# One encoder layer on one core: state-space rows without their 1 / rms, a written order of the output products and logits, and expert weights loaded from the first branch product on

## Chip, cores and metric

The kernel runs on one core of a Trainium2 chip, as one program and one launch. The metric is the device time of an execution in microseconds; each time is the median of several runs. The core has five engines that run side by side, each through its own list of instructions in order: TensorE (PE; its weight loads are PEld), VectorE (DVE), ScalarE (ACT), GpSimd (POOL) and SyncE (SP), which issues nearly all DMAs. Matrix products land in PSUM, eight banks of 128 rows of 512 fp32 values; everything else lies in SBUF.

## The reference

One layer of a streaming encoder on 256 tokens of width 1024, all in fp32. After a norm, one wide projection feeds two branches. One is sparse attention. The other is a state-space scan (SSD): 2048 channels in 4 groups, which is multiplied by SiLU of a gate z, normed within each group of 512 channels and scaled:

```python
yf = y * silu(z)
yg = yf.reshape(..., 4, 512)
yg = yg * rsqrt(mean(yg * yg, axis=-1) + 1e-6)
y_ssd = yg.reshape(..., 2048) * ssd_norm

merged = sigmoid(gate_a) * (y_attn @ w_attn_branch) + sigmoid(gate_b) * (y_ssd @ w_ssd_branch)
x = x + merged @ w_out
x = x + hier_moe(rmsnorm(x, ffn_norm), ...)
```

The last part routes each token to one of 4 expert groups and in it to 2 of 8 SwiGLU experts (hidden width 256). Every one of the 32 experts has weights of 3 MiB, 96 MiB in all.

## The kernel before

**Order of the work.** The program is written with a framework that plans the order of each engine's instructions from a simulated time line. Instructions of one engine may change places; where an order is wanted, it is forced by `pin` (behind everything written before on that engine), by `tc.issue_after(i)` (behind instruction i) and by a raised priority (`HP`).

**Weights of the dense part** come in 38 chunks of up to 8 slices of 128 rows. `next_w` asks for the next chunk one chunk ahead. SyncE loads it as raw fp32 (line 141) into 4 buffers "R"; ScalarE casts each slice to the high half (line 152), and GpSimd or VectorE, in turns, subtract it from the raw value for the low half (line 156), into buffers "S" that hold 6 slices. A product takes three passes: high by high, high by low, low by high (`PASSES`). `wide_chunk` multiplies both token tiles t = 0, 1 of 128 rows with 512 columns, 48 matmuls, into two PSUM banks; t = 1 runs `LAG` slices behind t = 0.

**State-space stage** (`ssd_x`, `ssd_e`, `ssd_y`, `ssd_tail`, lines 706 to 784). For each group g and half q, `ssd_y` computes yg, 256 channels by 256 tokens, with channels on the rows, and adds their squares into ysum. `ssd_tail(g)` sums ysum over the rows (ps_n), computes 1 / rms of each token as a column nv, turns that into a row that stands on all 128 partitions by two small matmuls with the identity (ps_r, line 775), multiplies yg by the gain and by that row, and splits it into the high and low half of yT[g] (lines 781 to 784). The four yT are held in the four large buffers "L".

**Branch products** (lines 825 to 847). Four chunks (i, c): i is the half of the channels (groups 2i and 2i + 1), c the half of the 1024 output columns. Each product, of 8 slices of channels in one sum, is multiplied by (gate table + 1) on its way out of PSUM (line 832) and added to `tab`, on GpSimd for i = 0, on VectorE for i = 1; then it is transposed into mT (tag "G").

**Output product and logits** (lines 869 to 912). w_out comes as one chunk of 512 columns and two of 256. For each slice c of 256 columns: x1 = x + product (VectorE), squares (ScalarE), two transposes for each token tile (ps_hf), a scaling to xT by ScalarE and VectorE, and the router's logits (ps_lg). The last slice is done by token tile. `warm2` puts matmuls with no use behind given instructions; 11 stand behind the last logit and 3 behind each rank.

**Routing and experts.** `route(t)` is a chain of some 13 VectorE operations with one small matmul (ps_rk) that ends in the slot matrix Dm. Eight passes q of 4 experts follow: `gather(k, n)` picks the tokens of slice k by matmuls with Dm (ps_g) and scales them into xg; `gate_up(k)` multiplies four experts at once into pgu; then the down product (py) and the sum over experts (acc). `GA` is the order of gathers and products in the first pass; `combine` computes the weights of the experts' outputs, and its VectorE work is queued behind the last Dm.

**Expert loads.** The weights are 96 tiles of 1 MiB, 12 in each pass. `prefetch(tags)` issues the next tiles on SyncE into buffers that are named by a letter: 7 E, 2 H, 2 A, 3 X, 4 L, 2 made of R, 3 of S and 2 of G, 25 in all, and then the same ring again. Each load is queued behind the last raw load that has been written, and waits for its buffer: X lies over memory of the state-space stage, L over the yT. Before: two X after chunk (1, 0), an X and an L after (1, 1), then an L with each of three slices of the output product; R, S and G come after the logits.

Of the kernel before, what the change touches and what calls it, by code (L numbers as in the profile page):

```python
# [20 lines left out]
P = 128  # L21
# [27 lines left out]
def block_kernel(ctx, tc, xin, idn, ngain, catt, cprep, cssd, cmoe, cwr, wsm, wwide, win, wgu, wdn, out, dbg=None):  # L49
# [185 lines left out]
    def mm3(regions):  # L235


        for k in range(KD):
            for j, (ps, lhs, rhs) in enumerate(regions):
                for i, (a, b) in enumerate(PASSES):  # L240
                    pe.matmul(ps, lhsT=lhs[k][:, a], rhs=rhs[k][:, b],  # L241
                              start=j == 0 and k == 0 and i == 0,
                              stop=j == len(regions) - 1 and k == KD - 1 and i == 2)

# [438 lines left out]
    snorm = C("snorm")  # L683
    yT = [bigt([P, 2, 4, T], F32R, f"yT{g}") for g in range(4)]
# [53 lines left out]
    def ssd_y(g, q):  # L738
# [3 lines left out]
        st_[g, q, "yg"] = yg  # L742
# [3 lines left out]
        for h2 in range(2):  # L746
# [9 lines left out]
            dve.tensor_tensor(yg[:, h2, :], yg[:, h2, :], zs[:, h2, :], op=ALU.mult)  # L756
        sq = zs_t[g, q]
# [7 lines left out]
    def ssd_tail(g):  # L765
# [4 lines left out]
        r = ssd.tile([P, 2], F32, tag="nv", name="nv")  # L770
# [6 lines left out]
        for q in range(2):  # L777
            yg = st_[g, q, "yg"]
            for b in range(2):
                ct = 4 * g + 2 * q + b  # L780
# [44 lines left out]

    for i in range(2):
        for c in range(2):
            ps = wide_chunk("S", yT[2 * i:2 * i + 2], LAG)
            for t in range(2):
# [16 lines left out]
            if i:  # L846
                prefetch(PF1[2 * c] + PF1[2 * c + 1])
# [21 lines left out]
    for c in range(4):  # L869
        if c == 0:  # L870
            pw = wide_chunk("o", mT, 4)
            for t in range(2):
                dve.scalar_tensor_tensor(x1[:, t, 0:512], pw[t], 0.5, x_sb[:, t, 0:512], op0=ALU.mult, op1=ALU.add)
        elif c == 2:
            ps = tm_chunk(next_w(), mT, "o")
        elif c == 3:
            ps = [pmm.tile([P, T], F32, tag="mm", name=f"ps_o{t}") for t in range(2)]
            regions = tm_regions(next_w(), mT, ps)
        prefetch(PFO[c])
        o = slice(256 * c, 256 * c + 256)  # L880
        if c == 3:

            dve.tensor_reduce(pre, ssq[:, :, 0:3], axis=AX.X, op=ALU.add)
            dve.tensor_scalar(pre, pre, D * EPS, None, op0=ALU.add)
        for ts in ((0,), (1,)) if c == 3 else ((0, 1),):
            tt = slice(ts[0], ts[-1] + 1)
            nt = len(ts)
            if c == 3:
                mm3(regions[ts[0]:ts[0] + 1])
            phf = pacc.tile([P, 2, nt, P], F32, tag=f"acc{ts[0]}1", name="ps_hf")  # L890
            xT = mo2.tile([P, 2, nt, P], F32, tag="y", name="xT")
            if c > 1:
                dve.scalar_tensor_tensor(x1[:, tt, o], ps[ts[0]].unsqueeze(1) if c == 3 else ps, 0.5, x_sb[:, tt, o],
                                         op0=ALU.mult, op1=ALU.add)
# [416 lines left out]
```

## Time and profile before

| | |
|---|---|
| median of 3 runs | 583.62 us (583.45 to 583.9) |
| profiled execution | 585.1 us |
| its span, first to last instruction | 583.3 us |
| busy: PE, DVE, ACT, POOL | 552.6, 330.9, 271.8, 239.5 us |
| read from device memory | 157.54 MB, 272 GB/s over the span |
| granted TensorE clock, mean | 0.987 |

The profile is of one execution. Busy time of TensorE is modelled: matmuls overlap, so a busy share near 1 means that no gap was seen. A DMA share of 1 means that the core's 16 DMA engines were all busy. Names are those of the program: ps_S is the branch product, ps_o the output product, ps_lg the logits, ps_hf the transposes ahead of them, ps_g the gather, pgu the expert product, we an expert tile, w_raw and w_hl the raw and the split dense weights. L156 is line 156 of the kernel; "<-" after an idle time names what ended it.

### The profile page before, as it was taken

The numbers are of one execution on the slowest core, as the hardware profiler recorded it, in microseconds if no ns is written. First come the engines' busy times: TensorE is split into PE (matmuls) and PEld (weight loads), VectorE is DVE, ScalarE is ACT, GpSimd is POOL, SyncE is SP. The second block draws the span as 40 slices with busy tenths as digits, with TensorE's granted clock in tenths as the row PEclk, the third lists the DMA queues.
The fourth block names the chain that finished last, engine by engine and source line by source line (L and its number), as shares of the span: only waits on it lengthen the run. The fifth ranks groups of instructions, "written<-read, shape, count | busy, mean of one in ns | idle before, by whom it ended". The sixth has DMA issues, their size and how long they took to land.

```text
span 583.3 us, 9898 instructions
## 1 busy us (share of the span) xinstructions
PE 552.6 (95%) x3605; PEld 400.6 (69%) x3605; DVE 330.9 (57%) x689; ACT 271.8 (47%) x633; POOL 239.5 (41%) x254
## 2 busy tenths in 40 slices
PE   8999989999999999999999999999998898988976
PEld 5878768798898999898878888964453452433512
DVE  3659975999996778989695657451111121111101
ACT  7567557757987877878764436410000000000001
POOL 4687584775844456656567745210000000000000
PEclk9999999999999999999999999999989997999989
DMA  7755244453435488645568589989999999999993
GB/s 272 250 162 169 103 147 146 144 174 124 128 122 186 149 323 334 217 149 185 208 194 300 177 307 389 405 344 417 419 417 408 420 417 421 409 415 421 420 407 123
DMA packets 35123, 159.27 MB, mean 273 GB/s; under 512 B 4096, under 2 KB 5760, under 8 KB 25856
## 3 DMA queue, kind: packets, MB, share of 16 engines
q1 hardware_dynamic: 33776, 157.30, 71.8%
q10 hardware_dynamic: 1296, 1.30, 0.7%
q8 instruction: 30, 0.49, 0.3%
q14 instruction: 21, 0.17, 0.1%
HBM read 157.54 MB, written 1.05 MB: 272 GB/s over the span
## 4 chain that ended last, share of the span: by engine, by line
PE 69%; DMA 12%; DVE 9%; issue 4%; POOL 3%; ACT 3%; SPq 0%; ACTq 0%; POOLq 0%; DVEq 0%
PE ps_S L294 8%; PE pgu L1037 6%; PE ps_xs L241 6%; PE ps_g L294 6%; DMA we<-wdn 5%; DMA we<-wgu 5%; PE ps_z L241 5%; PE py L1097 4%; PE ps_A L294 4%; PE acc L1112 4%; PE ps_g L1030 4%; PE ps_q L294 3%; PE ps_o L241 2%; PE ps_o L294 2%; PE ps_iq L294 2%
## 5 line engine op out<-in xcount | busy, mean ns | idle before, releaser
L156 POOL TENSOR_TENSOR w_hl<-w_raw,w_hl 128x512 fp32r<-128x512 f32 (+1 forms) x101 | 141.6, 1406 | 81.8 <-ACT w_hl L152 66.5
L152 ACT CAST w_hl<-w_raw 128x512 fp32r<-128x512 f32 (+1 forms) x212 | 125.7, 620 | 46.4 <-PE ps_S L294 18.5
L156 DVE TENSOR_TENSOR w_hl<-w_raw,w_hl 128x512 fp32r<-128x512 f32 (+1 forms) x111 | 100.4, 911 | 38.7 <-ACT w_hl L152 38.1
L1055 POOL TENSOR_TENSOR dc<-Dm,cmr 128x128 f32<-128x128 f32 x16 | 6.1, 401 | 143.5 <-DVE Dm L960 137.4
L1037 PE MATMUL pgu<-we,xg 128*32 128x512 f32 x512 | 60.2, 603 | 3.9 <-DMA we<-wgu 3.9
L241 PE MATMUL ps_z<-hT,w_hl 128*128 128x256 f32 x384 | 51.7, 286 | 0.0
L241 PE MATMUL ps_xs<-hT,w_hl 128*128 128x256 f32 x384 | 50.7, 285 | 0.0
L241 PEld LDWEIGHTS ps_z<-hT,w_hl 128*128 128x128 f32 x384 | 47.8, 190 | 2.0 <-issue 2.0
L241 PEld LDWEIGHTS ps_xs<-hT,w_hl 128*128 128x128 f32 x384 | 47.6, 191 | 2.1 <-issue 2.1
L294 PE MATMUL ps_g<-w_hl,gT 128*128 128x512 f32 x192 | 48.1, 399 | 0.0
L294 PE MATMUL ps_S<-w_hl,yT 128*128 128x512 f32 x192 | 44.6, 391 | 0.0
L1033 DVE TENSOR_TENSOR xg<-ps_g,cmoe 128x512 f32<-128x512 f32 (+2 forms) x18 | 11.3, 631 | 57.4 <-PE ps_g L1030 57.4
L1030 PEld LDWEIGHTS ps_g<-Dm,x_sb 128*128 128x128 f32 x256 | 31.0, 191 | 14.9 <-issue 9.7
L294 PEld LDWEIGHTS ps_g<-w_hl,gT 128*128 128x128 f32 x192 | 34.9, 188 | 9.3 <-DVE w_hl L156 1.0
L294 PEld LDWEIGHTS ps_S<-w_hl,yT 128*128 128x128 f32 x192 | 35.8, 188 | 7.4
L1037 PEld LDWEIGHTS pgu<-we,xg 128*32 128x32 f32 x512 | 15.1, 110 | 37.1 <-issue 26.1
L1097 PE MATMUL py<-we,aTt 128*32 128x512 f32 (+1 forms) x272 | 35.8, 616 | 3.8 <-DVE aTt L1083 2.1
L1108 ACT COPY y<-py 128x512 f32<-128x512 f32 (+1 forms) x9 | 4.8, 539 | 66.9 <-PE py L1097 66.9
L1075 DVE SCALAR_TENSOR_TENSOR ac<-th,pgu 128x256 f32<-128x256 f32 x8 | 3.4, 421 | 57.5 <-ACT th L1073 57.5
L1112 PE MATMUL acc<-y,dcT 128*128 128x512 f32 (+1 forms) x68 | 32.6, 606 | 0.9 <-DVE y L1110 0.8
L1030 PE MATMUL ps_g<-Dm,x_sb 128*128 128x128 f32 x256 | 33.4, 280 | 0.0
L1073 ACT ACTIVATE th<-pgu,rs 128x256 f32<-128x256 f32 x8 | 3.8, 474 | 55.1 <-PE pgu L1037 55.1
(296 smaller groups left out, 968.9 us busy)
## 6 DMA issues: line engine op xcount, KB each, us to landing
we<-wgu SPq DMA_DIRECT2D x55, 1024.0 KB, 13.8
w_raw<-wwide SPq DMA_DIRECT2D x60, 512.0 KB, 3.9
w_raw<-win SPq DMA_DIRECT2D x44, 512.0 KB, 3.9
we<-wdn SPq DMA_DIRECT2D x17, 1024.0 KB, 17.4
we<-wdn SPq DMA_DIRECT2D x28, 512.0 KB, 12.0
we<-wgu SPq DMA_DIRECT2D x18, 512.0 KB, 10.2
x_sb<-xin SPq DMA_DIRECT2D x2, 512.0 KB, 4.4
we<-wdn SPq DMA_DIRECT2D x4, 256.0 KB, 11.5
```

The source lines that it names most:

```text
L152: return act.copy(self.hl[i][:, 0], self.raw[i])
L156: return eng.tensor_sub(hl[:, 1], self.raw[i], hl[:, 0].bitcast(F32))
L241: pe.matmul(ps, lhsT=lhs[k][:, a], rhs=rhs[k][:, b], start=j == 0 and k == 0 and i == 0, stop=j == len(regions) - 1 and k == KD - 1 and i ...
L294: pe.matmul(ps[t], lhsT=lhs[t][k][:, a], rhs=w[k][:, b], start=k == 0 and i == 0, stop=k == KD - 1 and i == 2)
L1030: pe.matmul(ps[:, kk, :], lhsT=x1[:, t, (k + kk) * P:(k + kk + 1) * P], rhs=Dm[:, t].rearrange("p e j -> p (e j)"), start=t == 0, stop=t == 1)
L1033: dve.tensor_tensor(xg[:, ks, :], ps, fgain[:, ks].unsqueeze(2).to_broadcast([P, n, P]), op=ALU.mult)
L1037: i = pe.matmul(pgu[32 * e:32 * e + 32, :], lhsT=xg[:, k, 32 * e:32 * e + 32], rhs=wg[k][e], start=k == 0, stop=k == KD - 1, tile_position ...
L1055: pool.tensor_tensor(dc[:, t], Dm[:, t], cmr[:, t, 4 * q:4 * q + 4].unsqueeze(2).to_broadcast([P, 4, NSLOT]), op=ALU.mult)
L1073: act.activation(th, pgu[:, 0:256], AF.Tanh, scale=rs)
L1097: i_py = pe.matmul(py[32 * e:32 * e + 32, :], lhsT=aTt[:, f, 32 * e:32 * e + 32], rhs=wd[2 * n + f][e][:, c], start=f == 0, stop=f == 1, t ...
L1108: act.copy(y, py)
L1112: pe.matmul(acc[t][n][:, c], lhsT=dcT[:, t * P:(t + 1) * P], rhs=y, start=False, stop=q == 7 and c.stop == 512)
```

## The change

**1 / rms.** `ssd_tail` keeps the column only, in a small tile `rg` of all groups. `ssd_y` now makes both halves of yT itself, without 1 / rms, by four operations on ScalarE and four on VectorE for each group. The branch product keeps the two groups of a chunk apart, four PSUM banks instead of two, and 1 / rms is a factor of each row on the way out:

```diff
+        hl = yT[g][:, :, 2 * q:2 * q + 2]
+        for b in range(2):
+            ct = 4 * g + 2 * q + b
+            act.activation(hl[:, 0, b], yg[:, b], AF.Copy, scale=snorm[:, ct:ct + 1])
+            dve.scalar_tensor_tensor(hl[:, 1, b], yg[:, b], snorm[:, ct:ct + 1], hl[:, 0, b].bitcast(F32),
+                                     op0=ALU.mult, op1=ALU.subtract)
...
-        ps_r = paux.tile([P, T], F32, tag="n", bufs=1, name="ps_r")
-        for t in range(2):
-            pe.matmul(ps_r[:, t * P:(t + 1) * P], lhsT=r[:, t:t + 1].to_broadcast([P, P]), rhs=ident,
-                      start=True, stop=True)
...
-                dve.scalar_tensor_tensor(yg[:, b, :], yg[:, b, :], snorm[:, ct:ct + 1], ps_r, op0=ALU.mult, op1=ALU.mult)
-            hl = yT[g][:, :, 2 * q:2 * q + 2]
-            act.copy(hl[:, 0], yg)
-            dve.tensor_sub(hl[:, 1], yg, hl[:, 0].bitcast(F32))
...
+    for t in range(2):
+        for c in range(2):
+            pool.tensor_scalar(tab[t, c][:, 1], tab[t, c][:, 1], 1.0, None, op0=ALU.add)
...
+                    if kk % 4 == 0:
+                        pss[t, g] = (pacc.tile([P, 512], F32, tag=f"acc{t}1", name="ps_S") if g
+                                     else pmm.tile([P, 512], F32, tag="mm", name="ps_S"))
+                    for a, b in PASSES:
+                        pe.matmul(pss[t, g], lhsT=src[kk][:, a, t * P:(t + 1) * P], rhs=w[kk][:, b],
+                                  start=kk % 4 == 0 and (a, b) == PASSES[0], stop=kk % 4 == 3 and (a, b) == PASSES[2])
+            for g, t in ((0, 0), (0, 1), (1, 0), (1, 1)):
...
-                dve.scalar_tensor_tensor(m, tb, 1.0, ps[t], op0=ALU.add, op1=ALU.mult)
-                if i == 0:
+                dve.scalar_tensor_tensor(m, pss[t, g], rg[:, 2 * i + g, t:t + 1], tb, op0=ALU.mult, op1=ALU.mult)
+                if i == 0 or g == 0:
                     pool.tensor_add(ta, m, ta)
```

**Expert loads.** The tiles and the ring are the same; the places of the prefetches move:

```diff
-            if i:
-                prefetch(PF1[2 * c] + PF1[2 * c + 1])
+            prefetch(PF1[2 * i + c])
...
-PF1 = ("X", "X", "X", "L")
-PFO = ("L", "L", "L", "")
+PF1 = ("X", "X", "XLL", "L")
+PFO = ("L", "", "", "")
```

**Output product and logits.** The loop over slices becomes a written list. `mm3_by_k` yields after each slice and token tile, `some(mm, n)` runs n such steps of three matmuls, `x1_part` does the addition and the squares, `turn` the transposes and scalings, `logits` the logits; all TensorE instructions in it are pinned:

```diff
+    some(mm, 8)
+    turn(0, both)
+    x1_part(1, both, None)
+    some(mm, 4)
+    logits(0, both)
+    turn(1, both)
+    some(mm, 4)
+    x1_part(2, both, ps)
+    prefetch(PFO[1] + PFO[2])
...
+    mm = mm3_by_k(regions[0:1])
+    logits(1, both)
+    some(mm, 4)
+    turn(2, both)
...
+    some(mm, 4)
+    x1_part(3, (0,), pst[0].unsqueeze(1))
+    logits(2, both)
+    mm = mm3_by_k(regions[1:2])
+    some(mm, 4)
+    turn(3, (0,))
+    some(mm, 4)
+    logits(3, (0,))
+    x1_part(3, (1,), pst[1].unsqueeze(1))
+    turn(3, (1,))
+    last_lg = logits(3, (1,))
```

**First pass of the experts.** Slices 0 and 1 are gathered, then slice 0 is multiplied; each later gather is queued behind the product before it; the combine's VectorE work is queued behind the second gathered tile instead of the last Dm:

```diff
-            for k in GA:
-                gather(k[0], k[1])
-                for kk in range(*k[2:]):
-                    gate_up(kk)
+            gathered = [gather(0, 1), gather(1, 1)]
+            i_gu = gate_up(0)
+            for k, n, a, b in GA:
+                with tc.issue_after(i_gu.ins):
+                    gather(k, n)
+                for kk in range(a, b):
+                    i_gu = gate_up(kk)
...
-            with tc.issue_after(routed.ins):
+            with tc.issue_after(gathered[1].ins):
                 combine()
...
-GA = ((0, 1, 0, 0), (1, 1, 0, 1), (2, 2, 1, 2), (4, 4, 2, 4))
+GA = ((2, 2, 1, 2), (4, 4, 2, 4))
```

## Rows read from the trace of the kernel before

**Rows 1.** The chain that ended last, in order of time: start us, us, what.

```profile
322.38 25.65 PE ps_S L294 x113
...
498.98 11.39 DMA we<-wdn
```

**Rows 2.** Stretches by stage: busy us (count) by engine; then PEclk, DMA share, GB/s.

```profile
205.00:307.60 102.60, 102.44 (x758) 89.41 (x757) 90.90 (x151) 78.24 (x172) 64.74 (x55) 1.00 0.65 232
307.60:353.10 45.50, 45.50 (x210) 37.79 (x209) 26.70 (x39) 20.80 (x37) 28.13 (x23) 1.00 0.77 263
353.10:388.30 35.20, 34.94 (x241) 29.98 (x241) 21.53 (x69) 15.52 (x43) 11.45 (x12) 1.00 1.01 407
388.30:573.00 184.70, 166.52 (x1158) 72.58 (x1158) 30.48 (x72) 10.88 (x23) 6.04 (x16) 0.96 0.99 405
```

**Rows 3.** Waits of TensorE from 205 to 388 us: total us, times, longest.

```profile
PE ps_lg L911 <- ACT xT L907: 0.2, 1, 0.2
```

**Rows 4.** Stretches of 2 us about the first expert product; columns as above.

```profile
388.00:390.00 2.00, 2.00 (x17) 1.04 (x17) 0.75 (x3) 0.00 (x0) 0.76 (x2) 1.00 0.32 127
390.00:392.00 2.00, 2.00 (x17) 1.04 (x16) 0.00 (x0) 0.00 (x0) 0.00 (x0) 1.00 0.78 209
```

**Rows 5.** Waits of SyncE's queue from 386 us on: total us, times, longest.

```profile
SPq L270 <- DMA we<-wgu: 82.0, 46, 2.1
...
SPq L270 <- PE pgu L1037: 25.5, 18, 8.4
```

**Rows 6.** SyncE from 386 to 400 us: start, us, operation.

```profile
389.39 8.83 SPq L270 DMA_DIRECT2D we<-wgu  x7
```

**Rows 7.** Expert tiles from 386 to 396 us: issue to landing.

```profile
DMA to landing us min/median/max: 4.8/5.5/8.6
```

**Rows 8.** Timeline from 300 us: the last group's tail on TensorE.

```profile
321.78 0.61 PE L775 MATMUL ps_r<-ident,nv 128*128 128x128 f32 x4
...
322.14 25.90 PE L294 MATMUL ps_S<-w_hl,yT 128*128 128x512 f32 x113
```

**Rows 9.** Second branch chunk as a stretch; columns as above.

```profile
318.50:329.50 11.00, 11.00 (x52) 9.15 (x51) 9.36 (x13) 5.68 (x11) 8.00 (x7) 1.00 0.59 197
```

**Rows 10.** Low halves (line 156) from 205 to 353 us: ns min/median/max.

```profile
L156 DVE TENSOR_TENSOR w_hl<-w_raw,w_hl x41: 676/694/1782, 205.6 to 351.0; 128x512 fp32r<-128x512 f32 x41
L156 POOL TENSOR_TENSOR w_hl<-w_raw,w_hl x41: 1272/1363/1802, 210.2 to 351.6; 128x512 fp32r<-128x512 f32 x41
```

**Rows 11.** Timeline from 305 us, SyncE's queue.

```profile
337.84 1.24 SPq L270 DMA_DIRECT2D we<-wdn  x1
```

**Rows 12.** Timeline from 346 us: first output product's weights and matmuls.

```profile
350.37 1.14 ACT L152 CAST w_hl<-w_raw 128x512 fp32r<-128x512 f32 x2 [3.21 <-DMA w_raw<-wwide]
...
353.07 5.83 PE L294 MATMUL ps_o<-w_hl,mT 128*128 128x512 f32 x24
```

**Rows 13.** Timeline from 376 us, TensorE: last logits, warm-up, ranks, gathers.

```profile
379.86 0.98 PE L911 MATMUL ps_lg<-cwr,xT 128*128 128x36 f32 x8
...
381.54 1.14 PE L911 MATMUL ps_lg<-cwr,xT 128*128 128x36 f32 x8 [0.24 <-ACT xT L907]
382.51 2.54 PE L867 MATMUL ps_w<-on 128*128 128x512 bf16 x11
385.01 0.18 PE L954 MATMUL ps_rk<-sel,trs 128*128 128x32 bf16 x1
...
386.38 1.95 PE L1030 MATMUL ps_g<-Dm,x_sb 128*128 128x128 f32 x16
388.26 1.07 PE L1037 MATMUL pgu<-we,xg 128*32 128x512 f32 x8
389.26 1.60 PE L1030 MATMUL ps_g<-Dm,x_sb 128*128 128x128 f32 x12
```

**Rows 14.** Timeline from 386 us, VectorE: first operation after the slots, first gathered tile.

```profile
386.36 0.16 DVE L987 TENSOR_TENSOR ge<-logit,gm 128x8 f32<-128x8 f32 x1
...
387.25 0.29 DVE L1033 TENSOR_TENSOR xg<-ps_g,cmoe 128x128 f32<-128x128 f32 x1
```

More of the change, by code (lines that the diff above doesn't have):

```diff
@@ L243, in mm3, with mm3_by_k @@
                               stop=j == len(regions) - 1 and k == KD - 1 and i == 2)
+    def mm3_by_k(regions):
+        for k in range(KD):
+            for j, (ps, lhs, rhs) in enumerate(regions):
+                for i, (a, b) in enumerate(PASSES):
+                    pin(pe.matmul(ps, lhsT=lhs[k][:, a], rhs=rhs[k][:, b],
+                                  start=j == 0 and k == 0 and i == 0,
+                                  stop=j == len(regions) - 1 and k == KD - 1 and i == 2))
+                yield
     def pairs(tl, sl):
@@ L867, in warm2 @@
                 pe.matmul(ps_w, lhsT=on16, rhs=on16.unsqueeze(1).to_broadcast([P, 4, P]), start=True, stop=True)
[L869 to L879, printed above, removed]
+    phf, xTs = {}, {}
@@ L880, in block_kernel, with some, x1_part @@
+    def some(gen, n):
+        for _ in range(n):
+            next(gen, None)
+    def x1_part(c, ts, ps):
         o = slice(256 * c, 256 * c + 256)
[L881 to L885, printed above, removed]
+        if c > 1:
             tt = slice(ts[0], ts[-1] + 1)
[L887 to L894, printed above, removed]
[L895 to L912 removed]
@@ new lines, in x1_part, with turn @@
+            dve.scalar_tensor_tensor(x1[:, tt, o], ps, 0.5, x_sb[:, tt, o], op0=ALU.mult, op1=ALU.add)
+        for t in ts:
+            sq = mo2.tile([P, 256], F32, tag="dc", bufs=1, name="sqo")
+            act.activation(sq, x1[:, t, o], AF.Square, accum_out=ssq[:, t, c:c + 1])
+    def turn(c, ts):
+        nt = len(ts)
+        ph = pacc.tile([P, 2, nt, P], F32, tag=f"acc{(c + ts[0]) % 2}1", name="ps_hf")
+        xT = xTs[c, ts] = mo2.tile([P, 2, nt, P], F32, tag="y", name="xT")
+        for kk in range(2):
+            for t in ts:
+                k = 2 * c + kk
+                pin(pe.transpose(ph[:, kk, t - ts[0], :], x1[:, t, k * P:(k + 1) * P], ident))
+        for kk in range(2):
+            k = 2 * c + kk
+            if kk:
+                dve.tensor_scalar(xT[:, kk], ph[:, kk], fgain[:, k:k + 1], None, op0=ALU.mult)
+            else:
+                act.activation(xT[:, kk], ph[:, kk], AF.Copy, scale=fgain[:, k:k + 1])
@@ new lines, in logits @@
+    def logits(c, ts):
+        for kk in range(2):
+            for t in ts:
+                k = 2 * c + kk
+                i = pin(pe.matmul(ps_lg[t], lhsT=xTs[c, ts][:, kk, t - ts[0], :], rhs=wr[:, k, :],
+                                  start=k == 0, stop=k == KD - 1))
+        return i
+    both = (0, 1)
+    pw = wide_chunk("o", mT, 4)
+    for t in range(2):
+        dve.scalar_tensor_tensor(x1[:, t, 0:512], pw[t], 0.5, x_sb[:, t, 0:512], op0=ALU.mult, op1=ALU.add)
+    prefetch(PFO[0])
@@ new lines, in block_kernel @@
+    ps = pmm.tile([P, 2, T], F32, tag="mm", name="ps_o")
+    mm = mm3_by_k(tm_regions(next_w(), mT, [ps[:, t, :] for t in range(2)]))
+    x1_part(0, both, None)
+    some(mm, 8)
[7 more added lines that the diff above has]
+    prefetch(PFO[1] + PFO[2])
+    pst = [pmm.tile([P, T], F32, tag="mm", name=f"ps_o{t}") for t in range(2)]
+    regions = tm_regions(next_w(), mT, pst)
+    mm = mm3_by_k(regions[0:1])
```

39 lines of the change are left out of this document (14 added, 25 removed).

## Prediction

> **What bounds the kernel now.** I read the chain of waits first, in order of time. Up to about 497 us it is mostly TensorE, for instance 113 branch matmuls in one piece of 25.65 us, about 227 ns each; from 498.98 on it is the landing of expert tiles almost to the end [rows 1]. So the end is set by the stream of expert tiles, and the question is what sets the start of that stream. The stretches by stage show it: from 353.1 to 573 us the line carries 405 to 407 GB/s at a DMA share of 0.99 to 1.01, which is full; before that it is not (share 0.65 from 205 to 307.6, 0.77 from 307.6 to 353.1) [rows 2]. One tile is 1.05 MB, so 2.6 us at this rate; 184.7 us at 405 GB/s are 74.8 MB, which is the 71 of the 96 tiles that do not fit into the ring of 25.
>
> The 25 that fit are loaded before the first expert product, and the two stretches about that product show the hand-over: at 388 to 390 us the share falls to 0.32, at 390 to 392 it is 0.78 [rows 4]. The ring is full by then, and the next load needs a tile that the expert products give back: SyncE issues it at 389.39 [rows 6], and a tile lands 4.8 us after issue at the least [rows 7]. After that TensorE runs ahead of the line again: SyncE's queue waits 82.0 us in 46 waits for expert tiles of one kind alone, and only 25.5 us for matmuls [rows 5]. So the end moves with the first tile given back, as long as the 25 have landed by then. Today both happen within about a us of each other: an earlier load alone gains nothing, and an earlier product alone would run into loads that have not landed. The change moves both.
>
> What sets the first product? TensorE, without a gap: from 205 to 307.6 us it is busy 102.44 of 102.60, and in the branch products 45.50 of 45.50 [rows 2], and of the waits that the view lists from 205 to 388 us the longest is 0.2 us [rows 3]. So TensorE work taken out before 388 us moves the first product by its length, if the weights keep pace.
>
> **The change part by part.**
>
> *The 1 / rms row (gain 1.9 us).* Per group the two outer products into ps_r go. Four instructions start at 321.78, the next one 0.36 us later, and the last ends at 0.61 [rows 8]; four groups are 1.4 to 2.4 us of TensorE, I take 1.9. On VectorE four products with a PSUM operand and two 512-wide subtractions become four 256-wide operations, on ScalarE two 512-wide copies become four half-sized ones; VectorE is busy 90.90 of 102.60 and ScalarE 78.24 there [rows 2], so VectorE gets the room that it needs to hand out weights earlier, and ScalarE still has 24 us to spare. I cost this at nothing; if it fails, the gain is 0 and not less.
>
> *Four instead of two evictions in a branch product (loss 0.4, from 0 to 3).* TensorE does the same 48 matmuls per chunk, and VectorE's two extra evictions find it busy 26.70 of 45.50 [rows 2]. GpSimd is the thin place. In the second chunk it is busy 8.00 of 11.00 us [rows 9] with two adds; with four, at the 1.36 us of its other 512-wide operation of two operands [rows 10], that is 10.7. The third and fourth chunk get two more each as well. Its weight halves come just in time for TensorE, so a lag of more than about 2 us shows. Four additions of 1 to the gate are new too: their shape has no row, so 0.3 to 1.8 us each (nothing, to the slowest of rows 10). They depend on the gates alone, whose tables are ready long before, and can fill GpSimd's idle 38 us of the stage before (64.74 busy of 102.60 [rows 2]). If they stand in the first chunk instead, they are 1 to 7 us more of a queue that has none left. I take 0.4.
>
> The rows of line 156 say one thing more: the same VectorE subtraction, of one shape, takes 676 to 1782 ns [rows 10]. The Trainium skill (SBUF — State Buffer, section "Who interferes with whom") states that a VectorE operation with two SBUF inputs and a GpSimd operation that reads SBUF exclude each other for their whole length. By that rule every new add also holds up a subtraction, the two engines' times add up, and the sum would be that of rival A; the trace agrees as far as 676 against 1782 ns go.
>
> *Expert loads from the first branch chunk (0 by itself; loss 0.6, from 0 to 2.4).* Today the first tiles of this stretch go out at 337.84 [rows 11], behind the last branch weights; the line has 0.77 of its time used there [rows 2]. Two of them now go out one and two chunks earlier, into idle time, worth about 5 us of line: the 25 land that much sooner, and the hand-over then depends on the product alone. That is the cover for the rest of the sum. The price is in the third prefetch: three tiles instead of two stand ahead of the first output weights in SyncE's queue, 2.6 us more. Those weights are already late: ScalarE waited 3.21 us for them and began to cast at 350.37, and TensorE took up the output product at 353.07 [rows 12], with one cast (0.57) and one GpSimd half (1.36) in between; almost no slack. TensorE can use the halves of both token tiles as they come, and two earlier tiles have left the line, so not all of 2.6 us is lost. I take 0.6. The last two prefetches wait for branch rows that have been read by then; behind them stand only the later output weights, which come sooner.
>
> *Written order of output products and logits (loss 0.4, from -0.9 to 0.5).* Now 8 logit matmuls of the third slice and half of those of the fourth, with two transposes, stand behind the last output matmul (379.86 to 382.7 us) [rows 13]. Then they are in front of it, about 1.0 us of work moved, none removed; behind it stay four logit matmuls, the addition, two transposes and two scalings, which wait for each other. I count 0.8 us of gaps against today's 0.24 [rows 13], so the last logit comes 0.4 later. The routing of the first half of the tokens then overlaps, which would give back 0.8 to 1.3, but the 11 warm-up matmuls behind the last logit (2.54 us, and the first rank stands at 385.01, right at their end [rows 13]) stay in front of the ranks. So I expect the ranks 0.4 late.
>
> *Gathers (gain 0.9).* Today 16 gather matmuls run from 386.38 and the first expert product starts at 388.26 [rows 13]; the combine's VectorE work stands before the first gathered tile's eviction, which begins at 387.25 [rows 14]. After it, 8 matmuls (0.98) and an eviction of 0.29 stand before the product: 1.4 us with the latency instead of 1.88, a gain of 0.5 on the first tile given back. The second product waits for 8 gather matmuls instead of 12 (389.26 [rows 13]), and I give 0.4 more for the hole at 390 to 392 [rows 4]. Bounds 0 to 1.4. The combine comes later, but its result is wanted only after the products of this pass.
>
> *Sum.* -1.9 + 0.4 + 0.6 + 0.4 - 0.9 = -1.4 us. The profiled execution took 585.1 us for a span of 583.3; 583.7 is then its time after. The median of the runs is 583.62, 1.5 us under the profiled one, so I forecast 582.2.
>
> **The rivals.**
>
> *A, GpSimd binds the branch products (slower).* 8 adds at 1.36 and four additions of 1 put 12 to 18 us more on GpSimd within 45.5, its operations and VectorE's subtractions hold each other up, and TensorE waits for weight halves in the second and third chunk. For: 8.00 of 11.00 already busy, and 1782 against 676 ns. Against: TensorE had no wait at all there, and the additions can run before. It decides from a lag of about 2 us on; its price is 2 to 5 us, so with the other terms 0.2 to 3.2 slower: 584 to 587.
>
> *B, the output weights come too late.* The full 2.4 us are lost at 353 us and the tail's order costs its 0.5: -1.9 + 0.4 + 2.4 + 0.5 - 0.9 = +0.5, 584.1. For: ScalarE's wait of 3.21 us on that very load. Against: the two tiles taken out of the queue before.
>
> *C, the ranks come free of the warm-up, and nothing is late.* -1.9 + 0 + 0 - 0.9 - 1.4 = -4.2: 579.4. Against: the warm-up stands before the rank in the program and is ready first.
>
> *D, nothing moves.* The stream starts where it does because the line and not the product holds it: 583.6, give or take 0.6. For: both ends lie within a us. Against: the fall to 0.32.
>
> **How the numbers follow.** The forecast, from -0.4 to -3 (580.6 to 583.2), has 0.42; A 0.20; B 0.15; C 0.10; D 0.13. The order of all engines is planned anew, which may move any stage by a us, and that is in the widths. A measurement of this kernel tells 0.2%, 1.2 us, from no change. Faster by more: 0.28 of the forecast, C, and 0.03 of D, 0.41. Slower by more: 0.17 of A, 0.08 of B and 0.02 of D, 0.27. Within: 0.32. Leaving out half of C and the upper end of A, the range is 579.5 to 585.8; the forecast's own is 580.6 to 583.2.
>
> **What would show it.** Right: no ps_r; TensorE still without waits up to the ranks; first expert product about 1 to 2 us earlier; the DMA share low for longer before it, since the 25 land first; the same 184 us from there to the end. Wrong: TensorE waits for line 156 from GpSimd in the branch products (A), or for casts of the first output weights (B); ranks less than 2 us behind the last logit (C); a first product that is earlier by more than a us and an end that is not (D).

## The result: 5 us slower, and the profile after

The changed kernel takes 589.28 us (median of 6 runs, 589.06 to 590.98), the kernel before beside it 583.99 (6 runs, 583.45 to 586.37): a ratio of 1.0089, with a 95% interval of 1.0068 to 1.0109. The forecast was 582.2, the range ended at 585.8. The profiled execution took 589.06 us for a span of 587.3, 4.0 more than the span before. Two executions of all that follow, one of a_gat (620.48 us) and one of the kernel before (696.42), ran at a much lower granted clock (0.848 and 0.746) and are left out of the times given.

Stretches by stage come first, cut at the same events as [rows 2]. They are from the changed kernel; the columns are start and end, length, busy us (count) of PE, PEld, DVE, ACT and POOL, then PEclk, DMA share and GB/s.

```profile
205.00:306.00 101.00, 100.29 (x734) 87.17 (x732) 92.94 (x147) 79.21 (x179) 64.11 (x54) 1.00 0.63 228
306.00:353.40 47.40, 46.53 (x213) 37.13 (x211) 35.24 (x41) 18.47 (x32) 43.21 (x32) 1.00 0.85 311
353.40:391.60 38.20, 34.82 (x230) 29.11 (x228) 23.68 (x58) 16.72 (x43) 13.60 (x12) 1.00 0.83 286
391.60:577.00 185.40, 165.94 (x1164) 72.94 (x1165) 32.14 (x84) 11.35 (x26) 6.05 (x16) 0.97 1.01 410
```

The last stretch is as long as before (185.4 against 184.7 us) and as full: the expert stream still sets the end, and the loss lies ahead of it. TensorE stood for 0.2, 0.0 and 0.3 us in the three stretches ahead of it [rows 2]; now it stands for 0.7, 0.9 and 3.4. GpSimd is busy 43.21 of 47.40 us in the branch products, where it was 28.13 of 45.50. TensorE's own waits from 199 to 392 us (total us, times, longest) say for what:

```profile
PE ps_mT L862 <- DVE mg L859: 1.3, 1, 1.3
PE ps_o L304 <- ACT w_hl L152: 1.3, 1, 1.3
PE ps_n L786 <- POOL ysum L778: 0.9, 1, 0.9
PE ps_xs L241 <- DVE zs L713: 0.6, 1, 0.6
PE ps_lg L926 <- ACT xT L920: 0.5, 1, 0.5
PE pgu L1091 <- DVE xg L1087: 0.2, 1, 0.2
PE ps_hf L914 <- DVE x_sb L901: 0.2, 1, 0.2
```

Before there were two of 0.2 us from 199 to 389 us: the one in [rows 3], and one for acc, VectorE's convolution, which norow will meet again below (`PE ps_A L294 <- DVE acc L603: 0.2, 1, 0.2`). Four of the seven are waits for VectorE, two for ScalarE, one for GpSimd. Behind the first of the list stand the operations that the change added or slowed. In the same view of lines as [rows 10] (ns min/median/max, first and last start), of the changed kernel:

```profile
L857 POOL TENSOR_TENSOR tab<-mg,tab x12: 1283/1296/1745, 317.5 to 351.8; 128x512 f32<-128x512 f32 x12
...
L859 DVE TENSOR_TENSOR mg<-mg,tab x4: 1096/1770/1787, 345.3 to 361.0; 128x512 f32<-128x512 f32 x4
...
L156 DVE TENSOR_TENSOR w_hl<-w_raw,w_hl x40: 674/1042/1785, 205.0 to 348.0; 128x512 fp32r<-128x512 f32 x40
```

The addition on VectorE (line 859) in the kernel before:

```profile
L836 DVE TENSOR_TENSOR mg<-mg,tab x4: 679/932/1492, 342.8 to 357.5; 128x512 f32<-128x512 f32 x4
```

An addition on GpSimd takes 1.29 or 1.74 us, the addition on VectorE that the transposes into mT wait for 1.77 where it took 0.93 at the median, and VectorE's low halves 1042 ns at the median against 694 [rows 10]. Then the timeline of TensorE from 384 us (start, us, what), which answers [rows 13], and of SyncE from 392 us, which answers [rows 6]:

```profile
386.01 0.80 PE L926 MATMUL ps_lg<-cwr,xT 128*128 128x36 f32 x4 [0.46 <-ACT xT L920]
386.65 2.54 PE L889 MATMUL ps_w<-on 128*128 128x512 bf16 x11
389.02 0.18 PE L1008 MATMUL ps_rk<-sel,trs 128*128 128x32 bf16 x1
...
390.39 1.05 PE L1084 MATMUL ps_g<-Dm,x_sb 128*128 128x128 f32 x8
391.61 1.06 PE L1091 MATMUL pgu<-we,xg 128*32 128x512 f32 x8 [0.16 <-DVE xg L1087]
```

```profile
392.74 2.41 SPq L280 DMA_DIRECT2D we<-wgu  x2
```

The rank is 4.0 us later than before, the first expert product 3.35, since the gathers gave 0.66 back, where 0.5 was forecast (1.22 instead of 1.88 us from gather to product), and the first tile given back 3.35. That tile lands at 399.95, 7.2 us after its issue, 5.8 later than before: the last of the 25 lands only at 397.46 (390.38 before), and the line, full in the third stretch before, stood at a share of 0.83. The tile comes 2.49 us behind the last of the 25, where 3.79 us lay between the two before. Stretches about the first product of the changed kernel, columns as above:

```profile
391.00:393.00 2.00, 1.84 (x16) 0.81 (x15) 1.67 (x12) 0.49 (x3) 0.00 (x0) 1.00 1.00 404
393.00:395.00 2.00, 2.00 (x17) 1.04 (x17) 0.85 (x4) 0.00 (x0) 0.76 (x2) 1.00 1.05 426
```

Before, the share fell to 0.32 and 0.78 there [rows 4]. So the line has no hole at the hand-over any more: in the changed kernel the late filling of the ring, and not the first product, sets where the stream starts.

**A yardstick.** The profiled executions differ by up to 2 us before they reach anything that the change touches: the first prefix product (ps_cb, at the start of the state-space stage) stands at 199.1 us in the kernel before and at 198.5 in the changed one. So I measure every kernel from there: "branch" is the time to the start of the last branch matmul, "product" the time to the first expert product. Both come from starts in the trace, of one execution each, and half a us between two rows tells nothing: a_gat has the order of the kernel before on all engines up to the last branch matmul and reaches it 0.54 us later, and u_gat, the changed kernel up to the last logit, reaches that 0.55 later than the changed kernel. Summed for every TensorE operation up to the next one's start, the branch time splits exactly. From before to after, 153.78 to 154.93 us: ps_r goes (-2.09), behind the transposes ps_x and the broadcasts ps_b stand new gaps (+1.15 and +0.42), most of which end with results of VectorE (zs, and the convolution's acc), and the branch matmuls take 1.57 more, of which 1.03 are the wait for ysum. From there to the last logit: +3.58, of which 1.43 are the wait for the first output weights, 1.54 the holes around the transposes into mT, and 0.6 the logits' new order.

| kernel | branch | product | ratio to before (95% interval) |
|---|---|---|---|
| before | 153.78 | 189.19 | |
| changed | 154.93 | 193.15 | 1.0089 (1.0068 to 1.0109) |
| u_rms | 154.34 | 189.44 | 1.0017 (1.0004 to 1.0030) |
| u_pf | 154.94 | 193.87 | 1.0082 (1.0052 to 1.0112) |
| u_out | 154.94 | 193.86 | 1.0112 (1.0075 to 1.0148) |
| u_gat | 154.91 | 194.36 | 1.0097 (1.0076 to 1.0117) |
| adds_out | 154.71 | 191.37 | 1.0049 (1.0020 to 1.0078) |
| adds_dve | 154.72 | 191.49 | 1.0073 (1.0037 to 1.0108) |
| act_g0 | 154.73 | 193.90 | 1.0098 (1.0069 to 1.0127) |
| sqf | 156.49 | 194.37 | 1.0089 (1.0072 to 1.0106) |
| sqf_dve | 156.45 | 193.33 | 1.0074 (1.0045 to 1.0104) |
| combo | 155.50 | 191.12 | 1.0080 (1.0054 to 1.0105) |
| p4 | 154.81 | 189.93 | 1.0028 (1.0013 to 1.0043) |
| p8 | 157.66 | 193.05 | 1.0071 (1.0048 to 1.0094) |
| ev8 | 153.78 | 191.93 | 1.0037 (1.0016 to 1.0058) |
| p8ev8 | 157.14 | 192.50 | 1.0077 (1.0052 to 1.0102) |
| norow | 153.83 | 189.06 | 0.9996 (0.9978 to 1.0013) |
| a_gat | 154.32 | 188.88 | 0.9986 (0.9970 to 1.0002) |

### The profile page after: what moved, and what is told of

Its sections match the earlier page's. It is cut to its first block, busy times and chain, and to the rows that moved or that the text cites. A ratio compares the mean times of both kernels' runs of the same rounds, so it can differ in the third digit from the quotient of the medians.

```text
span 587.3 us, 9901 instructions
## 1 busy us (share of the span) xinstructions
PE 551.6 (94%) x3589; PEld 398.7 (68%) x3589; DVE 347.8 (59%) x689; ACT 271.8 (46%) x641; POOL 262.5 (45%) x266
## 4 chain that ended last, share of the span: by engine, by line
PE 48%; DVE 19%; DMA 17%; ACT 6%; issue 6%; POOL 4%; SPq 0%; ACTq 0%; POOLq 0%; DVEq 0%
DMA we<-wgu 9%; DMA we<-wdn 5%; PE pgu L1091 5%; PE ps_S L850 5%; DVE w_hl L156 4%; PE py L1155 3%; PE ps_z L241 3%; PE ps_xs L241 3%; PE ps_g L1084 3%; PE acc L1170 3%; PE ps_q L304 2%; PE ps_g L304 2%; DVE acc L613 2%; PE ps_o L250 2%; PE ps_iq L304 2%
## 5 line engine op out<-in xcount | busy, mean ns | idle before, releaser
L156 POOL TENSOR_TENSOR w_hl<-w_raw,w_hl 128x512 fp32r<-128x512 f32 (+1 forms) x101 | 145.1, 1443 | 61.8 <-ACT w_hl L152 49.4
L152 ACT CAST w_hl<-w_raw 128x512 fp32r<-128x512 f32 (+1 forms) x212 | 124.1, 620 | 46.4 <-PE ps_S L850 17.0
L156 DVE TENSOR_TENSOR w_hl<-w_raw,w_hl 128x512 fp32r<-128x512 f32 (+1 forms) x111 | 106.6, 969 | 22.4 <-ACT w_hl L152 21.8
L1170 PE MATMUL acc<-y,dcT 128*128 128x512 f32 (+1 forms) x68 | 30.6, 575 | 0.1
```

The lines of the kernel that those rows point to most:

```text
L152: return act.copy(self.hl[i][:, 0], self.raw[i])
L156: return eng.tensor_sub(hl[:, 1], self.raw[i], hl[:, 0].bitcast(F32))
L1170: pe.matmul(acc[t][n][:, c], lhsT=dcT[:, t * P:(t + 1) * P], rhs=y, start=False, stop=q == 7 and c.stop == 512)
```

## The experiments

### Which part: the four parts undone one at a time

u_pf puts the expert loads back, u_out the loop over output slices, u_rms the 1 / rms, u_gat the gathers; each edit is that part of the diff above, reversed.

> The changed kernel with the expert loads at their old places (two X after chunk (1, 0), X and L after (1, 1), then L, L, L with the output slices). Theory Q (queue): in the changed kernel three tiles stand ahead of the first output weights in SyncE's queue and the first of two L waits there for branch rows still being read (341.30 to 343.90), so these weights land 4 us later (354.3 to 358.1 instead of 350.3 to 354.1) and the output product starts 2.0 us later. Undone: first output product back at 353 to 354, time 586 to 587.5 against 589.3 changed and 584 before. Theory W (written order): the loss lies in the output product and logits; then 588.5 to 589.5. Theory G (GpSimd's additions): also 588.5 to 589.5.

> The changed kernel with the old loop over the output slices, which leaves the order of its TensorE instructions to the planner; all else as changed. Theory W: the pinned order lets no matmul of the third slice fill the holes of the wide product, which starts late and waits for its own rows and weights, and so costs 2 us from the first output product to the first rank (32 us before, 34 after); and it holds the buffers of split weights longer, so the last tiles of the ring are issued late. Undone: 585.5 to 587.3. Theory Q: the output weights are just as late, and the order matters little: 588.3 to 589.5. Theory G: 588.5 to 589.5.

> The changed kernel with 1 / rms put into the rows of yT as before (ps_r, two evictions in a branch product, no addition of 1 to the gates); all else as changed. Theory G: the eight extra GpSimd additions slow the weight halves and the last evictions (TensorE waits 1.3 us for mg and 0.9 us for ysum): undone 586.5 to 588. Theories Q and W: the 1.7 us that the branch products start earlier are used up by their own end (353.1 before, 353.6 after), so it makes no difference within 0.7 us: 588.6 to 590.

> The changed kernel with the old order of gathers and the old place of the combine. The first expert product follows the first gather by 1.88 us instead of 1.22. If the first tile given back sets the end, 589.7 to 590.5. If the fill of the ring sets it (the last of its 25 tiles lands at 397.5, after SyncE has issued the first tile given back at 392.7), the 0.66 us are hidden: 589.0 to 589.5.

Measured: 588.94, 589.79, 584.67 and 589.45 us, beside 583.67 before. Theories Q and W fall for either part by itself: undone alone, neither changes anything. Both effects are in the trace (in u_pf the first output product does begin 0.94 us sooner on the yardstick, 155.66 against 156.60), but its transposes into mT then wait 1.8 us for VectorE instead of 1.3, and the first expert product is no earlier. The whole loss follows the 1 / rms part. Without it GpSimd is back at 27.63 of 46.00 us in the branch products; stretches of u_rms, columns as above:

```profile
205.00:306.60 101.60, 101.42 (x750) 88.38 (x749) 90.47 (x152) 77.63 (x171) 64.80 (x55) 1.00 0.62 233
306.60:352.60 46.00, 45.80 (x209) 37.48 (x207) 29.44 (x41) 20.24 (x36) 27.63 (x22) 1.00 0.84 309
```

u_rms also says that the other three parts together bring nothing (+0.25 us to the first product, 1.0 us in time). In u_gat the product is 1.2 us later, about half of it the difference between executions named above, and the time the same within its interval; the first tile given back lands 2.49 us behind the last of the 25 there too, so the filling of the ring hides what the gathers give, as the second case of its expectation has it.

### GpSimd's additions and VectorE's evictions, taken from the changed kernel

adds_out leaves out those of group 0 (and so half of the sum), adds_dve moves them to VectorE:

```diff
-                if i == 0 or g == 0:
+                if g == 0:
+                    continue
+                if i == 0:
                     pool.tensor_add(ta, m, ta)
```

```diff
                 if i == 0 or g == 0:
-                    pool.tensor_add(ta, m, ta)
+                    (dve if g == 0 else pool).tensor_add(ta, m, ta)
```

> The changed kernel without the additions of group 0 of each branch product (that half of the sum is left out; its evictions stay). GpSimd then has 4 additions as before, VectorE as in the changed kernel. G1: the whole loss is gone and the 1.9 us of TensorE taken out show: 582 to 584. R: 588 to 589.5.

> The changed kernel with the additions of group 0 on VectorE instead of GpSimd (8 of 12). G1, only GpSimd's own time counts: POOL back to some 30 us in the branch products, 584 to 585.5. G2, GpSimd and VectorE operations on two SBUF inputs hold each other up, so the sum of both counts (in the trace an addition or a weight half on GpSimd takes 1.29 us alone and 1.74 beside such an operation): eight additions of 0.7 to 1.6 us on VectorE, 586 to 588. R: 588 to 589.5.

act_g0 sums the groups first:

```diff
...
+                    act.activation(ms[t], pss[t, g], AF.Copy, scale=rs)
+                    continue
+                m = ms[t]
+                dve.scalar_tensor_tensor(m, pss[t, g], rs, m, op0=ALU.mult, op1=ALU.add)
+                dve.scalar_tensor_tensor(m, tb, 1.0, m, op0=ALU.add, op1=ALU.mult)
```

> The changed kernel with the two groups summed ahead of the gate: ScalarE scales group 0 out of PSUM, VectorE adds group 1 times its 1 / rms, then (gate + 1) times that, then the addition as before; so no addition of 1 and 4 instead of 12 additions on GpSimd. ScalarE gets 8 operations of about 0.6 us (busy 17.9 of 46), VectorE 8 of about 1 us in place of 8 evictions of 0.74. G1: 582 to 584; G2: 583.5 to 585.5, since VectorE has eight more two-input operations than before; R: 588 to 589.5.

Measured: 586.35, 587.53 and 589.43 us, beside 583.53. Theory G1 is half right: without the additions, or with them on VectorE, the first product comes 1.8 and 1.7 us earlier, not 4. act_g0 shows why a relieved GpSimd is not enough: three dependent VectorE operations stand behind the last branch matmul, TensorE waits 1.6 us for mg and 1.2 for low halves, and all is lost again.

### The price alone, added to the kernel before

p_adds added the eight GpSimd operations in a form that changes values.

> The kernel before with nothing but eight more GpSimd additions of 128x512 in the branch products (each tab of the first half is added to once more, each of the second half to itself: the values are wrong, the operations are those of the changed kernel). Theory G1 (GpSimd's time: 42.1 of 46 us busy in the changed kernel's branch products, 28.5 before): eight times 1.3 to 1.75 us make the halves of the weights late, 586 to 588.5. Rival R (the rest of the 1 / rms edit costs it: rows written early, four PSUM banks, later evictions): 583.3 to 584.6.

Its values sent the program through its second path behind the routing (2048 matmuls into opg, which only that path has), so its 1331.6 us say nothing; up to the first expert product the trace can be read, and that stands 6.05 us later (195.24). So I put the same eight in a form that keeps the values, half of them, eight evictions, and both:

```diff
                 dve.scalar_tensor_tensor(m, tb, 1.0, ps[t], op0=ALU.add, op1=ALU.mult)
+                dve.scalar_tensor_tensor(m, tb, 1.0, ps[t], op0=ALU.add, op1=ALU.mult)
+                j = ta if i else m
+                pool.tensor_add(j, j, zc.to_broadcast([P, 512]))
```

The first added line is ev8, the other two are p8 (zc holds zeros), all three p8ev8; p4 is p8 for i = 0 alone.

> The kernel before with eight more GpSimd additions of 128x512 in the branch products (zero is added to the product's tile in the first half, to the table in the second; results as before). Theory G (GpSimd's queue): its 28.5 of 46 us become 41, TensorE waits for weight halves, the first expert product 3 to 6 us later: 586.5 to 589.5. Rival V (VectorE's evictions are the price): 583.5 to 584.8.

> As the run before, with the four additions of the first half only (chunks (0, 0) and (0, 1)). Theory G with a slack: GpSimd waits 14 of 46 us for ScalarE before, and a lag of 2 us is hidden, so four additions of 1.3 to 1.75 us cost less than half of eight: 583.8 to 585.5. If every addition costs its length (no slack): 586 to 587.

> The kernel before with each of the eight evictions of a branch product done twice on VectorE (the same result written again), 8 x 0.68 us. Theory G: VectorE has 19 of 46 us free there, 583.5 to 584.8. Theory V: VectorE's queue holds up the transposes into mT and the low halves, 585.5 to 587.5.

> Both together: the branch products' queues as in the changed kernel, with ps_r and all else as before. The loss of the changed kernel without what ps_r gives back would be some 4.9 + 2.1 us less what the other parts cost. If the two engines' queues are the whole price, 588.5 to 591; if the early split of the rows and the four PSUM banks cost as well, less than the changed kernel's: 585 to 588.

Measured: 588.18, 585.23, 585.65 and 587.99 us, beside 583.33. The stretch of the branch products of p8, and TensorE's waits from 199 to 392 us:

```profile
307.10:356.40 49.30, 46.40 (x209) 37.52 (x209) 33.70 (x43) 22.38 (x39) 40.86 (x33) 1.00 0.66 246
```

```profile
PE ps_S L294 <- POOL w_hl L156: 2.0, 2, 1.5
PE ps_S L294 <- DVE w_hl L156: 0.9, 1, 0.9
```

The same waits of ev8:

```profile
PE ps_o L294 <- DVE mg L833: 1.7, 1, 1.7
PE ps_o L294 <- DVE mT L846: 0.5, 1, 0.5
```

Two different prices in two places. The additions make weight halves late inside the branch products: the branch time grows by 1.03 us for four and 3.88 for eight, so there is a slack and it is used up between the two (theory G, and the slack, right), though the four that p4 lacks also stand in other chunks, and number and place are not told apart. The evictions cost nothing there (153.78, unchanged) and 2.7 us behind it. Theory V has the number right and the place wrong. Timeline of VectorE and TensorE in ev8:

```profile
356.83 1.27 DVE L833 SCALAR_TENSOR_TENSOR mg<-tab,ps_S 128x512 f32<-128x512 f32 x2
357.56 3.02 PE L294 MATMUL ps_o<-w_hl,mT 128*128 128x512 f32 x12 [1.68 <-DVE mg L833]
360.43 1.03 PE L840 MATMUL ps_mT<-ident,mg 128*128 128x128 f32 x8
```

What waits is the output product, and what it waits for is the repeated eviction itself, not the sum that the transposes need: ps_o takes its PSUM tiles from the same pool of three as ps_S, and the second token tile gets one only when line 833 has read it out. The changed kernel has no such wait in its list, so it doesn't pay these 2.7 us in that form. Together the two are not the sum, 3.9 + 2.7, but 3.3: p8ev8 comes to the output product 3.4 us late and has no wait for mg there. And 587.99 (587.10 to 589.57) is the upper edge of the second case of the last expectation, half a us below the first: it doesn't tell whether the two queues are the whole price.

### VectorE's queue in the state-space stage

sqf moves the squares ahead of the split in `ssd_y`; sqf_dve adds adds_dve to it; combo also takes back the output loop and the loads and gives the last evictions a higher priority.

```diff
-        hl = yT[g][:, :, 2 * q:2 * q + 2]
...
         sq = zs_t[g, q]
         act.activation(sq, yg, AF.Square)
...
+        hl = yT[g][:, :, 2 * q:2 * q + 2]
...
```

> The changed kernel with the squares and their sum ahead of the split of yT in the state-space stage; all else as changed. From the first prefix product to the last branch matmul the changed kernel takes 154.9 us, the kernel before 153.8, though 2.1 us of ps_r are gone: 1.6 us of it are TensorE's waits and gaps in the state-space stage, 1.0 its wait for the last sum of squares (ysum). Theory E (the early split stands in VectorE's and ScalarE's queues ahead of what TensorE waits for): the wait for ysum goes and part of the others, this stretch 152.9 to 154.0, time 587 to 588.5. Rival: the queues are as long in any order, or GpSimd's additions behind it eat the gain: 588.8 to 589.8.

> As the run before (squares first), and the additions of group 0 on VectorE. With the additions on VectorE alone the time was 587.5, and TensorE waited 1.6 us at the transposes into mT, 1.0 at ysum. Theory E: the two gains add up, 585.3 to 586.8. Rival (what is gained in front is lost at mT, whose rows come from VectorE's queue): 587 to 588.

> As the run before, and with the loop of output products and the places of the expert loads as in the kernel before, and a raised priority for the evictions of the last branch chunk: of the change only 1 / rms in the branch product and the gathers are left, the first with its queues relieved. If the loss of 1 / rms is queues alone, the 2.1 us of ps_r show: 582 to 584. If four evictions are too many for VectorE and GpSimd in whatever order, TensorE waits at mT again and the time is 584.5 to 587.

Measured: 589.91, 589.20 and 588.71 us, beside 584.16: theory E falls, and sqf_dve and combo lie above both of their cases. In sqf TensorE starts the branch products 1.9 us sooner than in the changed kernel and ends them 1.6 us later: it waits 1.3 us for a low half of VectorE 9 us into them, and after that its clock falls. Stretches of sqf, PEclk the third number from the end:

```profile
312.00:318.40 6.40, 5.11 (x17) 3.83 (x18) 3.38 (x5) 0.56 (x2) 6.29 (x6) 0.75 0.70 250
318.40:330.00 11.60, 11.60 (x52) 9.60 (x51) 8.97 (x10) 5.61 (x9) 9.69 (x7) 0.99 0.55 190
```

Behind two waits (0.7 us for ysum, 1.3 for the low half) the granted clock is 0.75 on the mean of this stretch, and seven branch matmuls start 0.43 us apart instead of 0.23, the lower of its two levels, which is 1.4 us of the loss. So an earlier start met weights that were not ready: at this place the halves, and not TensorE, set the pace. In combo nothing but 1 / rms and the gathers is left of the change, with the squares first and the additions of group 0 on VectorE, and still the product comes 2.2 us later than in a_gat.

### TensorE's work alone

norow takes ps_r out of the kernel before and adds nothing (it leaves out the right factor of each row); a_gat is the kernel before with the new gathers; row is a_gat with 1 / rms made as a row by one product and a wide power:

```diff
-        ps_r = paux.tile([P, T], F32, tag="n", bufs=1, name="ps_r")
-        for t in range(2):
-            pe.matmul(ps_r[:, t * P:(t + 1) * P], lhsT=r[:, t:t + 1].to_broadcast([P, P]), rhs=ident,
-                      start=True, stop=True)
...
-                dve.scalar_tensor_tensor(yg[:, b, :], yg[:, b, :], snorm[:, ct:ct + 1], ps_r, op0=ALU.mult, op1=ALU.mult)
+                dve.tensor_scalar(yg[:, b, :], yg[:, b, :], snorm[:, ct:ct + 1], r[:, 0:1], op0=ALU.mult, op1=ALU.mult)
```

```diff
-        for t in range(2):
-            pe.matmul(ps_n[:, t:t + 1], lhsT=ysum[:, t * P:(t + 1) * P], rhs=ones, start=t == 0, stop=t == 1)
-        r = ssd.tile([P, 2], F32, tag="nv", name="nv")
+        ps_n = paux.tile([P, T], F32, tag="n", bufs=1, name="ps_n")
+        pe.matmul(ps_n, lhsT=ones.to_broadcast([P, P]), rhs=ysum, start=True, stop=True)
+        r = ysum
```

> The kernel before without ps_r: the rows of yT are multiplied by the gain and by one column of 1 / rms (the wrong one, so this leaves out the right factor), with nothing added to any engine. If TensorE is the only bound up to the first product, this comes 2.1 us earlier (187.1 us after the first prefix product against 189.2) and the time is 581.3 to 582. Rival (the weight halves of GpSimd and VectorE bound the branch products as soon as TensorE begins them earlier): their end moves by less than 1 us and the time is 582.8 to 583.6.

> The kernel before with the new order of gathers and place of the combine alone. The first expert product follows the first gather by 1.2 us instead of 1.9 us (as in the changed kernel): 0.66 us earlier to the first tile given back. The fill of the ring ends 0.8 us before that today, so the gain is not hidden: 582.8 to 583.3 against 583.6. If the fill hides it: 583.5 to 583.8.

> The kernel before with the new gathers, and 1 / rms made as a row at once: one product of a block of ones with the sums of squares puts the sum on all rows, the power is taken of 128x256 on GpSimd, and ps_r goes. TensorE does some 1.5 to 2 us less, GpSimd four wider powers of about 1 to 3 us in place of 0.7 in the state-space stage, where it waits 38 of 102 us. If TensorE bounds: 581 to 582.5; if the weight halves do: 582.8 to 583.6; if the longer power delays the rows: 583.6 to 586.

norow measured 583.82 us beside 583.91: nothing. 2.09 us of TensorE's work are gone and the last branch matmul stands where it stood (153.83 against 153.78). Waits of TensorE in norow from 199 to 389 us, and the place:

```profile
PE ps_xs L241 <- DVE acc L603: 1.3, 1, 1.3
```

```profile
245.85 0.39 PE L752 MATMUL py<-e,xdt 128*64 128x128 f32 x4
247.56 1.70 PE L241 MATMUL ps_xs<-hT,w_hl 128*128 128x256 f32 x12 [1.32 <-DVE acc L603]
```

Halfway through the stage TensorE stands for VectorE's convolution (acc), which had kept just ahead of it before. TensorE's time on py, with the gaps behind it, is 1.9 us longer than before, 1.4 of it in this place, and that eats the saving. So the end of the branch products moves as little as the rival of the expectation has it, but the place is the state-space stage and not the weight halves. a_gat measured 583.69 beside 584.16; the product is 0.31 us earlier, and the interval of its ratio just reaches 1: it beats the changed kernel and is not told from the kernel before. Its first tile given back too lands 2.49 us behind the last of the 25, so the line leaves the gathers little to gain. row took 729.2 us, through its power on GpSimd (below).

## Why the prediction was wrong

**The step that failed** is the one that all others stood on: "So TensorE work taken out before 388 us moves the first product by its length, if the weights keep pace", with the 1 / rms row at a gain of 1.9 us and VectorE's part costed "at nothing". The 1.9 us of work were there (2.09 measured). Their gain was not, and norow shows it without any of the change's costs (its order of instructions is planned anew, which may have a share in the place of its wait). A stretch without gaps shows that nothing held TensorE up; it does not show by how much it may be sped up until something does. VectorE was busy 90.90 of 102.60 us there, and I read the 12 us of rest as room. They are an average: at some places VectorE hands its result over just as TensorE asks for it. The chain that ended last had said so before the forecast, which read it as "mostly TensorE" up to 497 us. In the kernel before (start us, us, what):

```profile
231.70 4.07 PE ps_z L241 x34
237.42 1.25 DVE yg L781 x3
...
276.45 1.69 DVE w_hl L156
278.59 3.24 PE ps_A L294 x13
```

From 237.0 to 278.6 us that chain runs through VectorE, and some GpSimd and ScalarE, and through no matmul, although TensorE shows no gap there. In the changed kernel the early split came on top (VectorE 92.94 of 101.00), and the stage had 1.6 us of new waits. The floor that I gave this term, "the gain is 0 and not less", was too high as well: ysum, one of the results behind the split, cost another 1.0 us.

**The four evictions** (loss 0.4, from 0 to 3): eight additions and eight evictions put behind the products of the kernel before (p8ev8) cost 3.3 us, above the upper bound. The bound was GpSimd's alone; VectorE's two more evictions were waved through with 26.70 of 45.50 us busy. In the changed kernel the price doesn't show where I looked for it: apart from the wait for ysum its branch products take 0.5 us more than before, which is no more than a_gat's do. It shows behind them, at the transposes into mT, where VectorE's last additions take 1.77 us each and stand one behind the other, with an eviction and a low half between them.

**Rival A** named GpSimd's load, and adds_out puts the additions of group 0 at 1.8 us of the product. But the sign given for it, TensorE waiting for line 156 in the branch products, is in p8's list and not in the changed kernel's. The sign of B is there, 1.3 us for a cast of the first output weights, and u_pf shows that taking it back gains nothing. Rival A came out at 584 to 587 only because it kept the 1.9 us of gain: its 2 to 5 us with the 0.6 + 0.4 - 0.9 of the other terms and no gain are 2.1 to 5.1 slower, and 5.3 were measured; since the place was another, that is in part luck. The rule of the Trainium skill (SBUF — State Buffer, section "Who interferes with whom"), that a VectorE operation with two SBUF inputs and a GpSimd operation that reads SBUF exclude each other, fits what the lines show, 1.29 or 1.74 us for the same addition and 0.67 to 1.79 for the same subtraction. How much of the loss is this and how much the queues' plain length no run here tells apart: the additions of group 0 cost 1.8 us on GpSimd (adds_out) and 0.1 on VectorE (adds_dve against adds_out), which fits both.

**The expert loads** (loss 0.6, from 0 to 2.4): the first output product did wait, 1.3 us, for ScalarE's cast of weights that landed late behind three tiles, where there was almost no slack. One of the three also waited 2.1 us in SyncE's queue for a buffer whose branch rows were still being read, which the forecast had left out. But taking it back gave nothing, since mg was later still. The cover that I named, "the 25 land that much sooner", failed: the last landed at 397.46, not at 390.38, as the tiles of the buffers R, S and G follow the output product.

**The written order** (loss 0.4) was 0.5 in u_rms and no more to be seen in u_out. **The gathers** (gain 0.9): 0.66 on the product and none of it at the end, because the condition of the forecast, "as long as the 25 have landed by then", failed.

**The product's 4.0 us by place.** The branch time is 1.15 longer, the way from there to the last logit 3.58, and from the last logit to the product 0.78 shorter. Against u_rms, which lacks the first two terms alone, it is 0.6 and 3.1. In the branch time ps_r gives 2.1 back, the new waits of the state-space stage take 1.6 and ysum 1.0. Behind it the wait for the first output weights takes 1.3, though the loads stand at the same places in both kernels, and the holes around the transposes 1.8. Of these 3.7 us the additions of group 0 carry 1.8 (adds_out). How the early split and the order of VectorE's queue share the rest stays open; such costs don't add up, as p8ev8 shows.

## What to carry to other kernels

Before a saving on the busiest engine is counted, look for who hands over to it last and how early: where the other engines' results arrive just in time, the saving is worth their slack and not its length, and leaving the work out for one run measures that. The chain that ended last can name that other engine, even where the busiest one shows no gap. Work moved from a busy engine to two that feed it has to be costed place by place, at the end of a stage above all, where the queues are drained in order and nothing is left to hide them. And two costs that lie one behind the other on the same chain don't add up, so a part undone alone can show nothing while it is late all the same.

## What was not expected of the hardware

A power on GpSimd costs by the column. In row, by line (ns min/median/max):

```profile
L100 POOL TENSOR_TENSOR ysum<-ysum,mhalf x4: 41122/41574/41598, 233.2 to 426.0; 128x256 f32<-128x256 f32 x4
L100 POOL TENSOR_TENSOR ss_q<-ss_q,mhalf x4: 1659/1888/2115, 68.0 to 146.3; 128x8 f32<-128x8 f32 x4
L100 POOL TENSOR_TENSOR rx<-rx,mhalf x2: 568/572/577, 6.2 to 7.5; 128x1 f32<-128x1 f32 x2
```

256 columns take 41.6 us, so 162 ns each, where an addition of the same 256 columns takes 0.74 (ysum, in the kernel before); my estimate of 1 to 3 us was worked out from the one of two columns at 0.71. The rows of one and of eight columns, 0.57 and 1.89 us, would have said it: 0.19 us for each column more.
